# The first modulation's matrix loaded ahead of the latents, and the tokens' norm summed by four groups of 128

## The chip, the cores and the metric

The kernel runs on one core of one Trainium2 chip. The metric is the device time of one execution in microseconds; the time given is the median of three runs. TensorE is called PE here, VectorE DVE, ScalarE ACT, GpSimd POOL and SyncE SP, as in the profile; PEld is PE's loading of weights.

## The reference

One layer of a block with two parallel mixers, for 512 latent tokens and 256 context tokens of width 2048. What stands at the kernel's start is this part:

```python
shift, scale, gate = jnp.split(silu(c) @ w_ada + b_ada, 3, axis=-1)
shift_c, scale_c, gate_c = jnp.split(silu(c_ctx) @ w_ada + b_ada, 3, axis=-1)
h = _rmsnorm(x, norm_g) * (1 + scale) + shift        # 512 x 2048
hc = _rmsnorm(ctx, norm_g) * (1 + scale_c) + shift_c
p = h @ w_in                                          # 2048 -> 9216
...
def _rmsnorm(x, g):
    return x * lax.rsqrt(jnp.mean(x * x, axis=-1, keepdims=True) + EPS) * g
```

Behind it come grouped-query attention over latents and context, a Fourier mix of 512 channels, gates, an output projection, a gated residual add and a last norm.

## The kernel before

Tokens lie along the free dimension, channels along the partitions: the latents are `xt`, 128 x 16 x 512 in f32, that is 16 blocks `kb` of 128 channels. Main products are f32 products made of three fp32r products each (`mm3`, L251 to L253): both operands are split into an upper half (`whi`, made on ACT, L131) and a lower half (`wlo`, made on DVE, L132).

The start works block by block. For block `kb`, `modulation(kb)` forms shift and gain of its 128 channels for latents and context: the two conditioning vectors `c2`, as 32 columns, times the block's columns of `w_ss` (`wa`, two tiles of 1 MB; 16 products at L425, four of them side by side in four groups of 32 columns). `columns` copies the result (L432, ACT), turns it (L435, PE) and adds the four groups up (L439, DVE); shift and gain follow (L487, L488, DVE). `make_h` then forms ht = xt x gain x rx (L414, DVE), its upper half (L415, ACT) and lower half (L416, DVE), and the block's main products with pieces of `w_start` can run (14 groups of three). `rx` is the tokens' inverse root mean square, the same for all channels of a token, kept on all 128 partitions.

`rx` comes from `squares`, called before the first modulation: each block of latents is squared (L394 on ACT, three of them L392 on DVE), pairs of blocks are added (L395, DVE), and eight products with a matrix of ones (L397, f32, 128 x 512) sum over channels into one bank of PSUM. Root (L404, ACT) and reciprocal (L405, DVE) work on 128 x 512. `warm` (L445) issues products whose results nobody reads.

Order is set by the queues. SP issues, in its program's order, the latents, the first modulation's matrix, first pieces of `w_start`, the second modulation's matrix, further pieces; POOL issues the matrices from the third on. `wa` has four buffers and the pieces of `w_start` four (`RAW`), so loads wait until their buffer's last reader is done. Each engine works through its own instructions in a fixed order, which a scheduler sets when the kernel is built. Behind the start everything else follows in the order of the code.

Of the kernel before, what the change touches and what calls it, by code (L numbers as in the profile page):

```python
# [10 lines left out]
F32 = mybir.dt.float32  # L11
F32R = mybir.dt.float32r
ACT = mybir.ActivationFunctionType
ALU = mybir.AluOpType
# [4 lines left out]
P = 128  # L19
D = 2048  # L20
T = 512
C = 256
KK = D // P
# [38 lines left out]
    f = {"P1": "Z5", "P2": "S2", "Q6": "S3", "P7": "S4"}.get(name)  # L62
    return [(f, pc - 1)] if f and g == 0 and pc in (1, 2) else []

XCH = [(0, 2), (2, 2), (4, 4), (8, 4), (12, 2), (14, 2)]


def start_pieces():
# [15 lines left out]
def block_kernel(ctx, tc, xT, ctxT, x, c_row, w_ss, w_gate, vecs, qkg, rope, dft_c, dft_s,  # L84
                 w_start, w_kv, w_m, w_g, w_pab, w_o, final_g, out):
    nc = tc.nc
    sb = lambda name, bufs=1, side="left": ctx.enter_context(tc.tile_pool(name=name, bufs=bufs, side=side))

    def region(name, side="left", **kw):
        st = ExitStack()  # L90
        return st, st.enter_context(tc.tile_pool(name=name, bufs=1, side=side, **kw))
# [18 lines left out]
    def uid(s):  # L110
        cnt[0] += 1
        return f"{s}{cnt[0]}"
# [3 lines left out]
    def slot(pool, shape, dt=F32):  # L116

        n = turns[pool] = turns.get(pool, -1) + 1
        return pool.tile([P] + list(shape), dt, tag=f"s{n % KK}", bufs=1, name=uid("s"))

    def hm_tile(shape, dt, name):
        return slot(hm, shape[1:], dt)

    def bank(shape=(P, 512)):
        return ps.tile(list(shape), F32, tag="b1", bufs=4, name=uid("pb"))

    def bank2():
        return ps.tile([P, 1024], F32, tag="b2", bufs=2, name=uid("pd"))
# [6 lines left out]
    todo, ahead = [], []  # L135
# [16 lines left out]
    def start_load():  # L152

        e = todo[0]
        used = [p for a in ahead for p, _ in a.raws]
        free = [p for p in raw_pools for _ in range(p[1] - used.count(p))]
        if len(e.parts) > len(free) or e.stage == 0 and (not chain or left[e.pc]):
            return False
        todo.pop(0)
        for p, src in zip(free, e.parts):  # L160
            raw = p[0].tile([P, 1024], F32, tag=p[2], bufs=p[3], name=uid("wr"))[:, : e.cols]
            nc.sync.dma_start(raw, src)
            e.raws.append((p, raw))
        if e.stage == 0:
            nc.sync.dma_start(chain[e.pc], e.first)
            left[e.pc] = 1
        ahead.append(e)
        return True
# [89 lines left out]
    ones = const.tile([P, P], F32, name="ones")  # L258
# [3 lines left out]
    eps_t = const.tile([P, 1], F32, name="eps_t")  # L262
# [4 lines left out]
    cvt, bada, ng = small[:, : 2 * KK], small[:, 2 * KK : 5 * KK], small[:, 5 * KK :]  # L267
# [8 lines left out]
    hhi = [None] * KK  # L276
    hlo = [None] * KK
# [51 lines left out]
    for g in range(4):  # L329
        for name in ONE_GROUP:  # L330
            stream_product(name, g, w_g[g], BY_DVE_GATES)
            if g >= 2 and name in DONE:
                half, c = DONE[name]
# [8 lines left out]
    for name in OUT_GROUP:  # L342
        stream_product(name, 4, w_o[1], BY_DVE_OUT)
        if name in DONE:
            half, c = DONE[name]
            stream(("x", half, 2 + c), flat(x[half, 2 + c]), 1024, 1, "raw")
    for name in ONE_GROUP:
        stream_product(name, 5, w_o[0], BY_DVE_OUT)
        half, c = {"P2": (0, 0), "P7": (1, 1), "Q3": (1, 0)}.get(name, (0, 0))
# [12 lines left out]
    pa, pap = region("pa", "right")  # L362
    xt = pap.tile([P, KK, T], F32, name="xt")

    def wada_load(kb, h):
        w = pap.tile([P, 8, 256], F32, tag="wada", bufs=4, name=uid("wa"))
        (nc.gpsimd if kb > 1 else nc.sync).dma_start(w, w_ss[kb, :, 8 * h : 8 * h + 8, :])
        return w

    for a, n in XCH:  # L370
        nc.sync.dma_start(xt[:, a : a + n, :], xT[:, a : a + n, :])


    c2 = pap.tile([P, KK, 32], F32, name="c2")
    nc.vector.memset(c2, 0.0)
    rt = pap.tile([P, 1], F32, name="rt")
    ce = pap.tile([P, 2 * KK], F32, name="ce")
    nc.scalar.activation(ce, cvt, ACT.Exp, scale=-1.0)
    nc.scalar.activation(rt, ce[:, 0:1], ACT.Sqrt)
    nc.vector.tensor_scalar(ce, ce, 1.0, None, op0=ALU.add)  # L380
    nc.vector.reciprocal(ce, ce)
    nc.vector.tensor_tensor(c2[:, :, 0:2].rearrange("p k j -> p j k"),
                            cvt.rearrange("p (j k) -> p j k", j=2),
                            ce.rearrange("p (j k) -> p j k", j=2), op=ALU.mult)
    def squares(srcs, n, r, new, run=None):

        acc = bank2()
        for q in range(0, KK, 2):
            a, b = new(), new()
            for t, src in zip((a, b), srcs(q)):  # L390
                if run is None and t is b and q in (4, 8, 10):
                    nc.vector.tensor_tensor(t, src, src, op=ALU.mult)  # L392
                else:
                    nc.scalar.activation(t, src, ACT.Square)  # L394
            nc.vector.tensor_tensor(a, a, b, op=ALU.add)  # L395
            if run is None:
                nc.tensor.matmul(acc[:, :n], ones, a, start=q == 0, stop=q == KK - 2)  # L397
            elif q == 0:
                nc.vector.tensor_copy(run, a)
            else:  # L400
                nc.vector.tensor_tensor(run, run, a, op=ALU.add)
        if run is not None:
            nc.tensor.matmul(acc[:, :n], ones, run, start=True, stop=True)
        nc.scalar.activation(r, acc[:, :n], ACT.Sqrt, bias=eps_t[:, 0:1], scale=1.0 / D)  # L404
        nc.vector.reciprocal(r, r)  # L405

    wada = {(0, h): wada_load(0, h) for h in range(2)}
    while todo and len(ahead) < 3:
        start_load()
    wada.update({(1, h): wada_load(1, h) for h in range(2)})  # L410

    def make_h(hi, lo, src, rr, kb, j, pool, n):
        tmp = pool.tile([P, n], F32, tag="htmp", bufs=2, name=uid("ht"))
        nc.vector.scalar_tensor_tensor(tmp, src, gain[:, kb, j : j + 1], rr, op0=ALU.mult, op1=ALU.mult)  # L414
        nc.scalar.activation(hi, tmp, ACT.Identity, bias=shift[:, kb, j : j + 1])  # L415
        nc.vector.scalar_tensor_tensor(lo, tmp, shift[:, kb, j : j + 1], hi.bitcast(F32),  # L416
                                       op0=ALU.add, op1=ALU.subtract)

    def matvec(acc, pieces):

        kk = 0
        for w in pieces:
            for k in range(w.shape[1]):
                j = kk % 4
                nc.tensor.matmul(acc[32 * j : 32 * j + 32, :256], c2[:, kk, :], w[:, k, :],  # L425
                                 start=kk < 4, stop=kk >= KK - 4)
                kk += 1

    def columns(acc, kb):

        o = pap.tile([P, 256], F32, tag="ada_o", bufs=2, name=uid("ado"))
        nc.scalar.copy(o, acc[:, :256])  # L432
        sp = acc[:, 512:768]
        for i in range(2):
            nc.tensor.transpose(sp[:, P * i : P * i + P], o[:, P * i : P * i + P], ident)  # L435
        if kb == 0:
            warm(5, o)
        r = pap.tile([P, 2, 2], F32, tag="ada_r", bufs=2, name=uid("adr"))
        nc.vector.tensor_reduce(r, sp.rearrange("p (h g r) -> p h r g", h=2, g=4)[:, :, 0:2, :], axis=AX.X, op=ALU.add)  # L439
        return r  # L440

    def warm(n, src):

        for _ in range(n):
            nc.tensor.matmul(wacc[:, :256], ones, src, start=True, stop=True)  # L445
# [35 lines left out]
    def modulation(kb):  # L481
        acc = bank2()
        matvec(acc, pieces := [wada.pop((kb, h), None) or wada_load(kb, h) for h in range(2)])
        if kb == 0:
            warm(3, pieces[1][:, 7, :])
        sp = columns(acc, kb)
        nc.vector.tensor_scalar(shift[:, kb, :], sp[:, 0, :], bada[:, kb : kb + 1], None, op0=ALU.add)  # L487
        nc.vector.tensor_scalar(gain[:, kb, :], sp[:, 1, :], bsc1[:, kb : kb + 1], ng[:, kb : kb + 1],  # L488
                                op0=ALU.add, op1=ALU.mult)

    wacc = bank()
    rx = pap.tile([P, T], F32, name="rx")
    squares(lambda q: (xt[:, q, :], xt[:, q + 1, :]), T, rx, lambda: hm_tile([P, 2, T], F32, name=uid("sq"))[:, 0, :])
    modulation(0)

    work = start_work()
    done = 0
    for kb in range(KK):
        if kb:
            modulation(kb)  # L500
        if kb % 2 == 0:
            pairs.append([hm_tile([P, 2, T], F32R, name=uid(n)) for n in ("hh", "hl")])
        hhi[kb], hlo[kb] = (t[:, kb % 2, :] for t in pairs[-1])
        make_h(hhi[kb], hlo[kb], xt[:, kb, :], rx, kb, 0, pap, T)

        full = max([k + n for k, n in GROUPS if k + n <= kb] or [0])
        owed = 42 * full
        lim = min(owed, done + 48)
        while done < lim:
            done += next(work)  # L510
# [88 lines left out]
    for g in range(4):  # L599
        gate_b(g)  # L600
        positions(g)
        if g < 2:
            channels(g + 2)
    squares(ct_load, C, rc, lambda: crp.tile([P, C], F32, tag="sq", bufs=4, name=uid("sq")),
            crp.tile([P, C], F32, name="run"))
    crs.close()
# [66 lines left out]
    for which, half in ((0, 0), (0, 1), (1, 1)):  # L673
        toks = range(3 * half, 3 * half + 3) if which == 0 else (4, 5)
        b = bank2()
        accs = [b[:, :512], b[:, 512:], bank()]
        for pc in range(8):
# [9 lines left out]
            if keys and pc in (1, 3, 5):  # L687
                a, t = keys.pop(0)
# [3 lines left out]
        for a, t in zip(accs, toks):  # L692
            a = a.rearrange("p (h d) -> p h d", h=4)
# [222 lines left out]
    acc = bank()  # L916
# [70 lines left out]
    for i in range(NSTEP + 2):  # L987
# [9 lines left out]
        if i % 3 > 0 and i < 3 * KK:  # L997
            q = i // 3 * 2 + i % 3 - 1
# [3 lines left out]
        if i % 3 < 2 and i < 3 * KK:  # L1002
            q = i // 3 * 2 + i % 3
# [354 lines left out]
```

## Time and profile before

| | |
|---|---|
| time, median of three runs | 1388.69 us (1388.03 to 1389.51) |
| the profiled execution | 1388.98 us |
| its span, first to last instruction | 1387.2 us |
| instructions | 17607 |
| loaded from HBM | 257.34 MB |
| written to HBM | 25.17 MB |
| mean granted clock of PE | 0.992 |

The profile is of one execution. A row of the timeline gives start, duration, engine, source line, operation, what is written and read, and how many instructions were merged into it; in brackets stands the idle time of the engine ahead of it and what ended it. The durations of PE's products overlap, since products are pipelined: how fast they follow each other is read from their starts. In rows of stretches, each engine's busy time is followed by its number of instructions, then the granted clock of PE, the busy share of the DMA engines, and GB/s. In rows of groups come the shapes, the count, busy us and mean ns of one, and idle time.

### The profile page before, as it was taken

How to read it: one execution, taken by the hardware profiler on the slowest of the kernel's cores; microseconds unless marked ns; L12 is line 12 of the kernel's file. 1: busy time of each engine (PE TensorE's matmuls, PEld its weight loads, DVE VectorE, ACT ScalarE, POOL GpSimd, SP SyncE). 2: the span in 40 equal slices, each digit the busy share in tenths (PEclk: the TensorE clock that was granted, in tenths of full speed). 3: DMA queues.
4: the chain of work that ended last, by engine and by line, in shares of the span. 5: the costliest groups of instructions: out<-in, count | busy, mean ns of one | idle time of the engine just before them, and what ended most of it. 6: DMA issues, size and time to landing. Idle time of an engine off the chain costs nothing. (4 is left out here: it accounts for less than half of the span.)

```text
span 1387.2 us, 17607 instructions
## 1 busy us (share of the span) xinstructions
PE 1351.4 (97%) x6810; PEld 1107.1 (80%) x6810; DVE 910.7 (66%) x1191; ACT 630.1 (45%) x861; POOL 116.8 (8%) x173
## 2 busy tenths in 40 slices
PE   7999999999999999999999999999999999999986
PEld 4667789888888888888887788888888788878865
DVE  5765486767865668656743776665956546487577
ACT  5322253534545454554544555444544224364434
POOL 0110000011100001000001101000010100020100
PEclk9999999999999999999999999999999999999998
DMA  9887453645443335433447998989898844588973
GB/s 384 330 343 263 168 186 108 185 122 186 153 145 113 116 113 161 140 98 121 124 143 271 326 291 239 258 226 258 263 269 296 310 152 136 136 184 274 238 220 131
DMA packets 76115, 283.67 MB, mean 204 GB/s; under 512 B 8704, under 2 KB 9344, under 8 KB 71680
## 3 DMA queue, kind: packets, MB, share of 16 engines
q1 hardware_dynamic: 52848, 185.28, 39.9%
q0 software_dynamic: 18000, 79.71, 21.2%
q10 hardware_dynamic: 5184, 17.57, 3.3%
q8 instruction: 53, 0.87, 0.3%
q14 instruction: 30, 0.25, 0.1%
HBM read 257.34 MB, written 25.17 MB: 204 GB/s over the span
## 5 line engine op out<-in xcount | busy, mean ns | idle before, releaser
L131 ACT ACTIVATE whi<-wr 128x1024 fp32r<-128x1024 f32 x178 | 185.0, 1043 | 292.7 <-PE pb L252 84.0
L132 DVE TENSOR_TENSOR wlo<-wr,whi 128x1024 fp32r<-128x1024 f32 x178 | 213.4, 1202 | 140.7 <-ACT whi L131 140.5
L251 PE MATMUL pb<-s,whi 128*128 128x512 f32 x512 | 206.7, 405 | 0.6 <-ACT s L415 0.6
L252 PE MATMUL pb<-s,whi 128*128 128x512 f32 x512 | 200.6, 392 | 0.1
L253 PE MATMUL pb<-s,wlo 128*128 128x512 f32 x512 | 200.5, 392 | 0.0
L252 PE MATMUL y<-wlo,s 128*128 128x512 f32 x320 | 127.2, 397 | 7.3 <-DVE wlo L132 7.2
L251 PE MATMUL x<-whi,s 128*128 128x512 f32 x324 | 127.3, 393 | 2.2 <-ACT whi L131 1.1
L252 PE MATMUL x<-wlo,s 128*128 128x512 f32 x324 | 127.2, 393 | 1.9 <-DVE wlo L132 1.9
L251 PE MATMUL y<-whi,s 128*128 128x512 f32 x320 | 126.8, 396 | 0.8 <-ACT whi L131 0.6
L253 PE MATMUL x<-whi,s 128*128 128x512 f32 x324 | 126.9, 392 | 0.0
L253 PE MATMUL y<-whi,s 128*128 128x512 f32 x320 | 126.4, 395 | 0.0
L251 PEld LDWEIGHTS pb<-s,whi 128*128 128x128 f32 x512 | 96.1, 188 | 21.7 <-issue 4.1
L253 PEld LDWEIGHTS pb<-s,wlo 128*128 128x128 f32 x512 | 96.1, 188 | 21.1 <-issue 0.4
L252 PEld LDWEIGHTS pb<-s,whi 128*128 128x128 f32 x512 | 96.4, 188 | 17.1 <-DVE s L416 1.0
L131 ACT ACTIVATE whi<-R 128x1024 fp32r<-128x1024 f32 x66 | 69.6, 1058 | 66.6 <-PE x L253 38.4
L132 DVE TENSOR_TENSOR wlo<-R,whi 128x1024 fp32r<-128x1024 f32 x66 | 80.0, 1219 | 20.5 <-ACT whi L131 20.4
L955 ACT ACTIVATE p<-pd,mx 128x768 f32<-128x768 f32 x48 | 43.2, 899 | 84.9 <-DVE mx L953 84.9
L252 PEld LDWEIGHTS y<-wlo,s 128*128 128x128 f32 x320 | 61.2, 191 | 22.9 <-DVE wlo L132 10.2
L251 PEld LDWEIGHTS x<-whi,s 128*128 128x128 f32 x324 | 61.3, 189 | 16.2 <-ACT whi L131 1.5
L252 PEld LDWEIGHTS x<-wlo,s 128*128 128x128 f32 x324 | 61.2, 189 | 15.2 <-DVE wlo L132 2.6
L251 PEld LDWEIGHTS y<-whi,s 128*128 128x128 f32 x320 | 61.1, 191 | 14.5 <-ACT whi L131 1.0
L253 PEld LDWEIGHTS x<-whi,s 128*128 128x128 f32 x324 | 61.3, 189 | 12.8
(270 smaller groups left out, 2663.7 us busy)
## 6 DMA issues: line engine op xcount, KB each, us to landing
wr<-in_w_g SPq DMA_DIRECT2D x80, 512.0 KB, 8.2
wa<-in_w_ss POOLq DMA_DIRECT2D x28, 1024.0 KB, 8.3
wr<-in_w_m SPq DMA_DIRECT2D x44, 512.0 KB, 3.8
wr<-in_w_gate SPq DMA_DIRECT2D x32, 512.0 KB, 3.6
wr<-in_w_pab SPq DMA_DIRECT2D x32, 512.0 KB, 4.3
R<-in_w_g POOLq DMA_DIRECT2D x32, 512.0 KB, 10.1
wr<-in_w_o SPq DMA_DIRECT2D x32, 512.0 KB, 5.2
wr<-in_w_start SPq DMA_DIRECT2D x26, 512.0 KB, 6.4
```

Of the source, the lines that this page charges most:

```text
L131: nc.scalar.activation(hi, src, ACT.Copy)
L132: nc.vector.tensor_tensor(lo, src, hi.bitcast(F32), op=ALU.subtract)
L251: nc.tensor.matmul(o, ah, bh, start=start, stop=False, skip_group_check=cont)
L252: nc.tensor.matmul(o, ah, bl, start=False, stop=False, skip_group_check=cont)
L253: nc.tensor.matmul(o, al, bh, start=False, stop=stop, skip_group_check=cont)
L955: nc.scalar.activation(p, sc[:, :NKEY], ACT.Exp, bias=mx[:, 0:1], accum_out=mx[:, 1:2])
```

## The change

The first modulation's matrix (two tiles of 1 MB) is loaded ahead of the latents; the latents' six loads are cut in other sizes; the second and the third modulation's matrix follow behind them on SP's queue, between pieces of `w_start` (the third was loaded by POOL before). `squares` stays for the context alone. For the tokens a new function, `token_norms`, sums squares in another way: each block's 512 squares are cut in four groups of 128 tokens, each multiplied with 32 columns of ones into its own 32 partitions of one bank, so that the sums fill 128 x 128 in place of 128 x 512; root and reciprocal work on that, and four products with a matrix that picks one row out of 32 spread the result back over 128 x 512. A filler product (`warm`) stands behind the sums of each of the first 14 blocks. The result stays in PSUM (`rx0`, read by the first block's `make_h`) and is copied to `rx` for the others. `modulation(0)` now stands ahead of the norm.

```diff
-XCH = [(0, 2), (2, 2), (4, 4), (8, 4), (12, 2), (14, 2)]
+XCH = [(0, 2), (2, 4), (6, 4), (10, 4), (14, 1), (15, 1)]
...
-        (nc.gpsimd if kb > 1 else nc.sync).dma_start(w, w_ss[kb, :, 8 * h : 8 * h + 8, :])
+        (nc.gpsimd if kb > 2 else nc.sync).dma_start(w, w_ss[kb, :, 8 * h : 8 * h + 8, :])
...
+    wada = {(0, h): wada_load(0, h) for h in range(2)}
     for a, n in XCH:
         nc.sync.dma_start(xt[:, a : a + n, :], xT[:, a : a + n, :])
+    start_load()
+    wada.update({(1, h): wada_load(1, h) for h in range(2)})
+    for _ in range(3):
+        start_load()
+    wada.update({(2, h): wada_load(2, h) for h in range(2)})
...
-    wada = {(0, h): wada_load(0, h) for h in range(2)}
-    while todo and len(ahead) < 3:
-        start_load()
-    wada.update({(1, h): wada_load(1, h) for h in range(2)})
+    def token_norms(rx):
+
+        t = hm_tile([P, 2, T], F32, name=uid("nm"))
+        pick, r = t[:, 0, :].rearrange("p (t c) -> p t c", t=4), t[:, 1, :P]
+        nc.gpsimd.memset(pick, 0.0)
+        for t in range(4):
+            nc.gpsimd.memset(pick[32 * t : 32 * t + 1, t, :], 1.0)
+        acc = bank()
+        for kb in range(KK):
+            if kb % 2 == 0:
+                two = hm_tile([P, 2, T], F32, name=uid("sq"))
+            sq = two[:, kb % 2, :]
+            if kb % 3 == 2 or kb == KK - 2:
+                nc.vector.tensor_tensor(sq, xt[:, kb, :], xt[:, kb, :], op=ALU.mult)
+            else:
+                nc.scalar.activation(sq, xt[:, kb, :], ACT.Square)
+
+            for t in range(4):
+                nc.tensor.matmul(acc[32 * t : 32 * t + 32, :P], ones[:, :32], sq[:, t * P : t * P + P],
+                                 start=kb == 0, stop=kb == KK - 1)
+            if kb < KK - 2:
+                warm(1, sq[:, :256])
+        nc.scalar.activation(r, acc[:, :P], ACT.Sqrt, bias=eps_t[:, 0:1], scale=1.0 / D)
+        nc.vector.reciprocal(r, r)
+        acc = bank()
+        for t in range(4):
+            nc.tensor.matmul(acc[:, t * P : t * P + P], pick[:, t, :], r, start=True, stop=True)
+        nc.scalar.copy(rx, acc)
+        return acc
...
-    squares(lambda q: (xt[:, q, :], xt[:, q + 1, :]), T, rx, lambda: hm_tile([P, 2, T], F32, name=uid("sq"))[:, 0, :])
     modulation(0)
+    rx0 = token_norms(rx)
...
-        make_h(hhi[kb], hlo[kb], xt[:, kb, :], rx, kb, 0, pap, T)
+        make_h(hhi[kb], hlo[kb], xt[:, kb, :], rx if kb else rx0, kb, 0, pap, T)
```

The conditioning vectors' exponential also gets a tile of its own (`ex`), so that the steps behind it on DVE need not wait for the reading that loads ACT's table of roots. In the changed kernel the lines of `modulation`, `columns`, `warm`, `make_h` and what follows them are 26 higher (L425 is L451, L445 is L471, L435 is L461); the norm's sums are L426, its root L430, its reciprocal L431, the products that spread it L434.

How the change moves instructions is shown at three places. First SP's queue from the program's start (`xt` are the latents, `wa` the modulations' matrices, `wr` the pieces of `w_start`). Before:

```order
L371 DMA xt<-in_xT 128x1024 x2
L371 DMA xt<-in_xT 128x2048 x2
L371 DMA xt<-in_xT 128x1024 x2
L367 DMA wa_127<-in_w_ss 128x2048
L367 DMA wa_129<-in_w_ss 128x2048
L162 DMA wr_131<-in_w_start 128x1024
L162 DMA wr_133<-in_w_start 128x256
L162 DMA wr_135<-in_w_start 128x512
L367 DMA wa_137<-in_w_ss 128x2048
L367 DMA wa_139<-in_w_ss 128x2048
L162 DMA wr_262<-in_w_start 128x1024
```

And now:

```order
L367 DMA wa_112<-in_w_ss 128x2048
L367 DMA wa_114<-in_w_ss 128x2048
L372 DMA xt<-in_xT 128x1024
L372 DMA xt<-in_xT 128x2048 x3
L372 DMA xt<-in_xT 128x512 x2
L162 DMA wr_122<-in_w_start 128x1024
L367 DMA wa_124<-in_w_ss 128x2048
L367 DMA wa_126<-in_w_ss 128x2048
L162 DMA wr_128<-in_w_start 128x256
L162 DMA wr_130<-in_w_start 128x512
L162 DMA wr_132<-in_w_start 128x1024
L367 DMA wa_134<-in_w_ss 128x2048
```

The first matrix moved ahead of the latents, and one more matrix (`wa_134` and the one behind it) stands on this queue.

Second PE, from its first product to the first main product (`pd` and `pb` are banks of PSUM, `s` a tile of squares, or in L251 the block's upper half). Before:

```order
L397 MATMUL pd_143<-s_180,ones 128x512
L397 MATMUL pd_143<-s_186,ones 128x512
L425 MATMUL pd_194<-wa_127,c_118 32x256 x8
L425 MATMUL pd_194<-wa_129,c_118 32x256 x8
L445 MATMUL pb_141<-wa_129,ones 128x256 x3
L435 MATMUL pd_194<-ident,ado_214 128x128 x2
L445 MATMUL pb_141<-ado_214,ones 128x256 x5
L425 MATMUL pd_233<-wa_137,c_118 32x256 x8
L251 MATMUL pb_276<-s_227,whi_264 128x512
```

Six more L397 stand ahead of these. Now the first rows are:

```order
L451 MATMUL pd_150<-wa_112,c_138 32x256 x8
L451 MATMUL pd_150<-wa_114,c_138 32x256 x8
L471 MATMUL pb_148<-wa_114,ones 128x256 x3
L461 MATMUL pd_150<-ident,ado_170 128x128 x2
L471 MATMUL pb_148<-ado_170,ones 128x256 x5
L426 MATMUL pb_189<-s_190,ones 32x128 x4
L471 MATMUL pb_148<-s_190,ones 128x256
L426 MATMUL pb_189<-s_190,ones 32x128 x4
```

After twelve more such pairs of L471 and L426, the stretch ends with these rows:

```order
L471 MATMUL pb_148<-s_268,ones 128x256
L426 MATMUL pb_189<-s_281,ones 32x128 x8
L434 MATMUL pb_294<-s_183 128x128 x4
L451 MATMUL pd_306<-wa_124,c_138 32x256 x8
L251 MATMUL pb_347<-s_300,whi_335 128x512
L451 MATMUL pd_306<-wa_126,c_138 32x256 x8
L252 MATMUL pb_347<-s_301,whi_335 128x512
```

The first modulation moved ahead of the sums of squares, whose small products alternate with fillers, and the second half of the second modulation moved up to right behind the first main product.

Third DVE, from the reciprocal to the first block's lower half (`wlo` is the lower half of a piece of weights, `adr` the modulation's sums). Before:

```order
L405 RECIPROCAL rx<-rx 128x512
L132 TENSOR_TENSOR wlo_265<-wr_131,whi_264 128x1024
L439 TENSOR_REDUCE adr_223<-pd_194 128x4
L132 TENSOR_TENSOR wlo_269<-wr_133,whi_268 128x256
L487 TENSOR_SCALAR shift<-adr_223,small 128x2
L488 TENSOR_SCALAR gain<-adr_223,bsc_93,small 128x2
L132 TENSOR_TENSOR wlo_273<-wr_135,whi_272 128x512
L414 SCALAR_TENSOR_TENSOR ht_229<-xt,gain,rx 128x512
L416 SCALAR_TENSOR_TENSOR s_228<-ht_229,shift,s_227 128x512
```

And now:

```order
L421 TENSOR_TENSOR s_281<-xt 128x512
L132 TENSOR_TENSOR wlo_336<-wr_122,whi_335 128x1024
L431 RECIPROCAL s_183<-s_183 128x128
L440 SCALAR_TENSOR_TENSOR ht_302<-xt,gain,pb_294 128x512
L442 SCALAR_TENSOR_TENSOR s_301<-ht_302,shift,s_300 128x512
L132 TENSOR_TENSOR wlo_340<-wr_128,whi_339 128x256
```

The lower half of the first piece now stands ahead of the reciprocal, the other two behind the block's lower half, and shift and gain went up ahead of the squares. On ACT, in the same way, the upper half of that first piece (L131) now stands ahead of the root (L430).

More of the change, by code (lines that the diff above doesn't have):

```diff
@@ L376, in block_kernel @@
     rt = pap.tile([P, 1], F32, name="rt")
+    ex = pap.tile([P, 2 * KK], F32, name="ex")
     ce = pap.tile([P, 2 * KK], F32, name="ce")
-    nc.scalar.activation(ce, cvt, ACT.Exp, scale=-1.0)
-    nc.scalar.activation(rt, ce[:, 0:1], ACT.Sqrt)
-    nc.vector.tensor_scalar(ce, ce, 1.0, None, op0=ALU.add)
+    nc.scalar.activation(ex, cvt, ACT.Exp, scale=-1.0)
+    nc.scalar.activation(rt, ex[:, 0:1], ACT.Sqrt)
+    nc.vector.tensor_scalar(ce, ex, 1.0, None, op0=ALU.add)
     nc.vector.reciprocal(ce, ce)
@@ L384, in block_kernel, with squares @@
                             ce.rearrange("p (j k) -> p j k", j=2), op=ALU.mult)
-    def squares(srcs, n, r, new, run=None):
+    def squares(srcs, n, r, new, run):
         acc = bank2()
@@ L390, in squares @@
             for t, src in zip((a, b), srcs(q)):
[L391 to L394, printed above, removed]
+                nc.scalar.activation(t, src, ACT.Square)
             nc.vector.tensor_tensor(a, a, b, op=ALU.add)
-            if run is None:
-                nc.tensor.matmul(acc[:, :n], ones, a, start=q == 0, stop=q == KK - 2)
-            elif q == 0:
+            if q == 0:
                 nc.vector.tensor_copy(run, a)
@@ L401, in squares @@
                 nc.vector.tensor_tensor(run, run, a, op=ALU.add)
-        if run is not None:
-            nc.tensor.matmul(acc[:, :n], ones, run, start=True, stop=True)
+        nc.tensor.matmul(acc[:, :n], ones, run, start=True, stop=True)
         nc.scalar.activation(r, acc[:, :n], ACT.Sqrt, bias=eps_t[:, 0:1], scale=1.0 / D)
         nc.vector.reciprocal(r, r)
-    wada = {(0, h): wada_load(0, h) for h in range(2)}
-    while todo and len(ahead) < 3:
-        start_load()
-    wada.update({(1, h): wada_load(1, h) for h in range(2)})
+    def token_norms(rx):
[25 more added lines that the diff above has]
+        return acc
     def make_h(hi, lo, src, rr, kb, j, pool, n):
```

## The prediction

> **What bounds the kernel now.** I read first the page's part 1, then busy time by stretches, then the timeline of the first 40 us.
>
> ```profile
> PE 1351.4 (97%) x6810; PEld 1107.1 (80%) x6810; DVE 910.7 (66%) x1191; ACT 630.1 (45%) x861; POOL 116.8 (8%) x173
> 25.60:200.00 174.40, 172.86 (x1091) 127.29 (x1092) 110.86 (x187) 60.50 (x92) 13.50 (x26) 1.00 0.72 265
> ```
>
> TensorE (PE) bounds everything behind the start: in the 174.40 us from its first main product on it is busy for 172.86. So what moves that first product (L251 at 25.61 us) moves the end nearly one for one. The start itself:
>
> ```profile
> 5.18 0.63 ACT L394 ACTIVATE s<-xt 128x512 f32<-128x512 f32 x1 [2.46 <-DMA xt<-in_xT]
> 8.63 8.99 PE L397 MATMUL pd<-s,ones 128*128 128x512 f32 x16 [8.63 <-DVE s L395]
> 13.91 1.15 ACT L394 ACTIVATE s<-xt 128x512 f32<-128x512 f32 x2
> 17.66 0.69 ACT L404 ACTIVATE rx<-pd,eps_t 128x512 f32<-128x512 f32 x1 [2.60 <-PE pd L397]
> 18.38 3.35 DVE L405 RECIPROCAL rx<-rx 128x512 f32<-128x512 f32 x1 [2.59 <-ACT rx L404]
> 18.87 1.07 PE L425 MATMUL pd<-wa,c 128*32 128x256 f32 x16 [0.25 <-DMA wa<-in_w_ss]
> 19.87 1.56 PE L445 MATMUL pb<-wa,ones 128*128 128x256 f32 x6
> 20.00 0.37 ACT L432 COPY ado<-pd 128x256 f32<-128x256 f32 x1 [1.66 <-PE pd L425]
> 20.27 1.89 ACT L131 ACTIVATE whi<-wr 128x1024 fp32r<-128x1024 f32 x3
> 21.27 0.38 PE L435 MATMUL pd<-ident,ado 128*128 128x128 f32 x2
> 21.48 2.32 PE L445 MATMUL pb<-ado,ones 128*128 128x256 f32 x10
> 21.65 1.16 DVE L132 TENSOR_TENSOR wlo<-wr,whi 128x1024 fp32r<-128x1024 f32 x1
> 24.06 0.74 DVE L414 SCALAR_TENSOR_TENSOR ht<-xt,gain,rx 128x512 f32<-128x512 f32 x1
> 24.84 0.72 ACT L415 ACTIVATE s<-ht,shift 128x512 fp32r<-128x512 f32 x1 [2.68 <-DVE ht L414]
> 25.61 0.73 PE L251 MATMUL pb<-s,whi 128*128 128x512 f32 x2 [0.59 <-ACT s L415]
> 28.93 1.07 PE L425 MATMUL pd<-wa,c 128*32 128x256 f32 x16 [0.42 <-DMA wa<-in_w_ss]
> ```
>
> Latents are squared as they land (last at 13.9), VectorE (DVE) then has the reciprocal (3.35), a split of weights and the first modulation's last steps in one row until ht at 24.06. An f32 product shows as two records: eight L397 are x16.
>
> **The part that decides: PE's time for the norm.** The squares' sums become, for each of 16 blocks of latents, four products with 32 columns (L426) and, for the first 14, one filler over the full array (L471, the old L445's shape). The fillers stand between the sums in PE's order, so PE changes between 32-column and full-width work 28 times. What one such change costs stands in the trace:
>
> ```profile
> 17.55 0.42 PE L425 MATMUL pd<-wa,c 128*32 128x256 f32 x4
> 17.79 0.13 PEld L425 LDWEIGHTS pd<-wa,c 128*32 128x32 f32 x4
> 18.00 0.61 PE L425 MATMUL pd<-wa,c 128*32 128x256 f32 x8
> 19.54 0.40 PE L425 MATMUL pd<-wa,c 128*32 128x256 f32 x4
> 19.87 0.48 PE L445 MATMUL pb<-wa,ones 128*128 128x256 f32 x1
> 19.87 0.19 PEld L445 LDWEIGHTS pb<-wa,ones 128*128 128x128 f32 x1 [0.41 <-issue]
> 19.87 0.70 PE L445 MATMUL pb<-wa,ones 128*128 128x256 f32 x2
> 36.87 0.39 PE L251 MATMUL pb<-whi,s 128*128 128x512 f32 x1
> 37.10 0.39 PE L252 MATMUL pb<-wlo,s 128*128 128x512 f32 x1
> 37.32 0.39 PE L253 MATMUL pb<-whi,s 128*128 128x512 f32 x1
> 37.64 1.93 PE L425 MATMUL pd<-wa,c 128*32 128x256 f32 x32
> 39.51 0.50 PE L251 MATMUL pb<-s,whi 128*128 128x512 f32 x1
> 39.84 0.40 PE L252 MATMUL pb<-s,whi 128*128 128x512 f32 x1
> ```
>
> Four 32-column records run side by side as a round; a round of 256 columns takes about 0.22 us (17.55 to 18.00 is two), so one of 128 columns 0.11. Same-width products follow each other at 0.23 (36.87, 37.10, 37.32). From full to 32 columns it is 0.32 (37.32 to 37.64). From 32 columns to full, the load of weights begins 0.33 after the last round (19.54 to 19.87), having idled 0.41; the first filler record then takes 0.32 (the x6 at 19.87 lasts 1.56, its first two 0.70, so 0.215 a record; L435 follows 1.40 after it, which leaves 0.32 for the first). Loads are not drawn ahead across the change. One block of latents: two rounds of 128 columns apart by 0.14 (0.11, and the 0.03 by which 17.79 lies behind 17.55 plus 0.22), then 0.22 to the filler (0.33 less 0.11 for the shorter stream), 0.32 in the filler, 0.32 back: **1.00 us**. Streaming alone would be 0.11 x 2 + 0.22 x 2, some 0.64. Latents come faster:
>
> ```profile
> 0.00:5.00 5.00, 0.00 (x0) 0.00 (x0) 0.89 (x6) 1.51 (x2) 0.68 (x6) 1.00 0.57 173
> 5.00:10.00 5.00, 1.37 (x2) 0.82 (x3) 2.38 (x6) 4.73 (x9) 0.00 (x0) 1.00 1.02 419
> 10.00:15.00 5.00, 5.00 (x10) 2.04 (x9) 4.51 (x8) 4.00 (x8) 0.00 (x0) 1.00 1.02 424
> ```
>
> At 419 GB/s a block (0.26 MB) takes 0.63. The first 0.86 MB pass by 5.0, and the first latents (0.57 MB with the vectors) are used at 5.18, so use lags the bytes by some 0.8. The first modulation's two halves (1.10 and 2.15 MB) are thus there at 6.4 and 8.9, the last latents, at the same 6.34 MB in all as before, near 18.8, their squares by 19.9.
>
> **When PE can begin.** In PE's order the first modulation and its fillers, moved whole ahead of the sums, stand first: L425's second half to the end of ten fillers, 18.87 to 23.65 (21.48, nine pitches and one stream of 0.22), 4.8 us. Now it starts at 8.9 on a cold array:
>
> ```profile
> 11.35 0.34 PEld L397 LDWEIGHTS pd<-s,ones 128*128 128x128 f32 x1 [0.52 <-DVE s L395]
> 12.20 0.29 PEld L397 LDWEIGHTS pd<-s,ones 128*128 128x128 f32 x1 [0.52 <-issue]
> 12.74 0.19 PEld L397 LDWEIGHTS pd<-s,ones 128*128 128x128 f32 x1 [0.24 <-issue]
> 13.17 0.19 PEld L397 LDWEIGHTS pd<-s,ones 128*128 128x128 f32 x1 [0.24 <-issue]
> ```
>
> The pitch halves from 0.85 to 0.43 near 12.3, 3.6 us after PE's first product at 8.63 (the granted clock reads 1.00 throughout, so it does not show this). Full pace from 12.4, 3.5 us into the new row: 3.5 us do 1.75 us of work, 3.05 remain, PE is free at **15.4**. Opening at 10.0 (3.6 after the first half) gives 14.3; at 13.4 gives 16.0. The Trainium skill, "TensorE: Matmul & The Clock Gate", Part 1 (the HAM clock gate), says that the array runs at half rate until a window of some 3.4 us was busy, and that these windows run free of the kernel's start. The trace's 3.6 fits; by the page alone the opening could come up to a window later, which as an estimate adds under 2 us.
>
> **The chain, and the sum.** 14 blocks at 1.00: 29.4. The last two without filler are four rounds at 0.14, the last record lasting 0.27 (see L435 below): 30.1. Root of 128x128: between nothing and 0.69, taken at 0.25 by the nearest rows (0.37 for 256 elements, 0.69 for 512): 30.4. The reciprocal:
>
> ```profile
> L381 DVE RECIPROCAL ce<-ce 128x32 f32<-128x32 f32 x1 | 0.4, 353 | 0.0
> L435 PE MATMUL pd<-ident,ado 128*128 128x128 f32 x10 | 2.0, 277 | 0.0
> ```
>
> From 0.35 at 32 elements and 3.35 at 512, a line gives 0.95 at 128 (bounds 0.35 and 3.35): 31.4 with handoffs of 0.05. L434's four products, eight records at L435's pitch of 0.11 (0.38 less 0.27), the last lasting 0.27: 32.5. Then ht 0.75 and its rounding 0.73, with handoffs: L251 at **34.1, 8.5 later**.
>
> Costs beside this: the 0.6 us copy of rx runs beside ht, and without that cover would add 0.6. Five memsets of GpSimd (POOL) run while it idles, before any root; uncovered, under 1 us. Eight DVE adds (L395), the old sums and 2.4 us of reciprocal go, but what is late next is PE's row, so nothing is credited. On ScalarE (ACT) and DVE the first weights' split now stands ahead of root and reciprocal; those weights are next on the queue behind 18.8, so it is done near 22.5, hidden under PE's row to 30.1 (if PE were early it would cost, see below). The SP queue takes two more issues of 1 MB, behind them the second block's pieces, needed near 45; POOL's remaining loads still wait for the modulation two before. At 0.42 MB a us behind 18.8, the second matrix lands near 25 (2.6 MB more with the first weights) and the third near 32 (3.0 more); PE needs them at 32.8 and 45.
>
> That gives something back. The first block's products took 25.61 to 37.64, 12.03. Now half a modulation fills the wait for the lower half, and no load is late (28.93 waited 0.42): 0.32 to it, 1.00 through it (as 18.87 to 19.87), 0.33, 39 pitches of 0.225, 0.32 out, transposes 0.2: 11.0, **1.0 less** (bounds 0 and 1.3).
>
> Sum: 8.5 - 1.0 = +7.5. The profiled execution took 1388.98 (span 1387.2), 0.29 above the median shown, 1388.69. Forecast **1396.5**. Its own bounds: start -1.1/+0.6, blocks 0.92 to 1.10 us (-1.1/+1.4), chain and give-back +-1.3: 1393 to 1399.8.
>
> **Rivals.**
> 1. Loads are drawn ahead: the blocks take 0.64, 14 x 0.36 = 5.0 less, 1391.5. Against it stand the idle loads at 19.87 and the 0.32 steps; for it, that same-width loads do overlap. The Trainium skill, "TensorE: Matmul & The Clock Gate", section "Step-by-step: what each phase is for", says weights are loaded ahead of running products where row groups do not conflict or the spare weight buffer is the target; by that the change of width would be free, which the 0.41 idle does not bear out.
> 2. Not slower: latents, not PE, pace the norm. Squares end at 19.9, the split (ACT from 20.2, 1.05; DVE to 22.4) holds root and reciprocal, then reciprocal 23.4, L434 24.5, ht 25.3, L251 26.05: +0.45 - 1.0, 1388.4. It decides only if PE needs under (19.9 - 15.4) / 16 = 0.28 us a block, below its 0.64 of streaming.
> 3. The array stays at half pace, since a third of each block is idle: the row of 4.8 takes 9.6 (18.5), blocks 2.0, the two blocks behind and L434 twice as long, L251 some 18.5 later still: 1415. After 12.3 the trace shows no return to the 0.85 pitch, though gaps of half a microsecond occur.
>
> **How the numbers follow.** Forecast 0.77, rival 1 0.12, rival 2 0.05, rival 3 0.06. A measurement of this kernel can tell about 0.2% (2.8 us) from no change. Slower by that (over 1391.5): the forecast, rival 3 and a little under half of rival 1, 0.87; same 0.11; faster 0.02. The range takes in rival 1 and leaves out rivals 2 and 3 and thin ends: 1391 to 1400.
>
> **What would show it.** Right: L426 starts near 15.4, repeats each 1.0 us with fillers between, ends near 30; DVE and ACT idle from 22.5 until the root near 30; L251 near 34; no DMA wait before L451's next halves; PE dense from there. Wrong: L426 blocks at 0.6 us, a root right behind the split near 21, fillers at 0.85, or a hole in PE past 36.

## The result, and the profile after

| | before | after |
|---|---|---|
| time, median (range; runs) | 1388.36 us (1386.47 to 1389.51; 4) | 1401.77 us (1399.64 to 1403.79; 4) |
| ratio to before, with its 95% interval | | 1.0095 (1.0078 to 1.0112) |
| the profiled execution, its span | 1388.98, 1387.2 | 1402.09, 1400.3 |
| products of PE (records) | 6810 | 6958 |

The changed kernel is slower, as forecast, but by 13.1 us between the profiled executions in place of 7.5; its median lies 1.77 above the top of the range. First the page's row of PE and a stretch of 174.40 us from the first main product on, to be held against the same length before:

```profile
PE 1360.0 (97%) x6958; PEld 1112.8 (79%) x6958; DVE 905.9 (65%) x1185; ACT 628.9 (45%) x860; POOL 117.1 (8%) x176
34.95:209.35 174.40, 173.30 (x1095) 128.41 (x1096) 112.62 (x190) 61.63 (x95) 13.24 (x25) 1.00 0.69 250
```

PE is as dense there as before (173.30 against 172.86), so nothing is lost in this stretch. The start, picked rows of the changed kernel's timeline (start, duration, engine, line, operation, what is written and read, instructions merged, and in brackets the idle time ahead and its end):

```profile
6.58 1.94 PE L451 MATMUL pd<-wa,c 128*32 128x256 f32 x16 [6.58 <-DMA wa<-in_w_ss]
8.97 1.93 PE L451 MATMUL pd<-wa,c 128*32 128x256 f32 x16 [0.45 <-DMA wa<-in_w_ss]
...
13.36 2.32 PE L471 MATMUL pb<-ado,ones 128*128 128x256 f32 x10
...
15.61 0.43 PE L426 MATMUL pb<-s,ones 128*32 128x128 f32 x8
15.97 0.30 PEld L471 LDWEIGHTS pb<-s,ones 128*128 128x128 f32 x2 [0.20 <-issue]
15.97 0.70 PE L471 MATMUL pb<-s,ones 128*128 128x256 f32 x2
16.60 0.42 PE L426 MATMUL pb<-s,ones 128*32 128x128 f32 x8
16.95 0.70 PE L471 MATMUL pb<-s,ones 128*128 128x256 f32 x2
...
29.40 0.64 PE L426 MATMUL pb<-s,ones 128*32 128x128 f32 x16
30.11 0.37 ACT L430 ACTIVATE s<-pb,eps_t 128x128 f32<-128x128 f32 x1 [8.75 <-PE pb L426]
30.52 0.95 DVE L431 RECIPROCAL s<-s 128x128 f32<-128x128 f32 x1 [7.90 <-ACT s L430]
31.61 1.13 PE L434 MATMUL pb<-s 128*128 128x128 f32 x8 [1.57 <-DVE s L431]
...
32.78 0.59 ACT L435 COPY rx<-pb 128x512 f32<-128x512 f32 x1 [2.30 <-PE pb L434]
33.40 0.75 DVE L440 SCALAR_TENSOR_TENSOR ht<-xt,gain,pb 128x512 f32<-128x512 f32 x1 [1.93 <-ACT rx L435]
34.18 0.72 ACT L441 ACTIVATE s<-ht,shift 128x512 fp32r<-128x512 f32 x1 [0.82 <-DVE ht L440]
34.96 0.49 PE L251 MATMUL pb<-s,whi 128*128 128x512 f32 x1 [1.21 <-ACT s L441]
...
48.01 0.50 PE L251 MATMUL pb<-s,whi 128*128 128x512 f32 x1
```

The blocks of the norm follow each other at 0.985 us (15.61, 16.60, and 29.40 after fourteen), paced by PE, with each load of weights idle for 0.20 or 0.33 at a change of width. The first main product comes at 34.96, 9.35 later than before (25.61), the second block's at 48.01, 8.50 later than before (39.51). Held against the kernel before product by product, the lag stays at 8.5 from there to 700 us. So far this is the forecast. The rest comes far behind the start. Stretches of ten us, the kernel before:

```profile
1060.00:1070.00 10.00, 10.00 (x46) 8.28 (x45) 7.80 (x9) 6.43 (x8) 0.00 (x0) 1.00 0.97 338
1070.00:1080.00 10.00, 10.00 (x46) 8.29 (x45) 4.34 (x4) 1.89 (x3) 0.00 (x0) 1.00 0.99 351
1080.00:1090.00 10.00, 8.49 (x30) 6.27 (x29) 5.86 (x5) 4.66 (x5) 0.00 (x0) 0.83 0.72 247
```

And the changed kernel, with its timeline from 1064 us on (`y` is a bank, `wr<-at_d` a piece of the attention's output that is loaded back from HBM):

```profile
1060.00:1070.00 10.00, 7.31 (x27) 5.45 (x27) 6.31 (x7) 3.90 (x4) 0.00 (x0) 0.87 0.51 161
1070.00:1080.00 10.00, 10.00 (x37) 8.01 (x36) 8.64 (x10) 6.10 (x8) 0.00 (x0) 0.79 0.99 334
1080.00:1090.00 10.00, 10.00 (x46) 8.29 (x45) 5.85 (x5) 4.02 (x4) 0.00 (x0) 1.00 0.90 334
```

```profile
1064.63 0.39 PE L253 MATMUL y<-s,s 128*128 128x512 f32 x1
1064.69 1.06 ACT L131 ACTIVATE s<-wr 128x1024 fp32r<-128x1024 f32 x1 [5.79 <-DMA wr<-at_d]
1065.65 1.99 ACT L131 ACTIVATE whi<-wr 128x1024 fp32r<-128x1024 f32 x2
1066.75 0.49 PE L251 MATMUL y<-whi,s 128*128 128x512 f32 x1 [1.73 <-ACT whi L131]
1068.20 0.79 PE L252 MATMUL y<-wlo,s 128*128 128x512 f32 x1 [0.95 <-DVE wlo L132]
1068.79 0.63 PE L253 MATMUL y<-whi,s 128*128 128x512 f32 x1
1069.22 0.63 PE L251 MATMUL y<-whi,s 128*128 128x512 f32 x1
```

PE waits for one load, idles 1.9 and 1.2 us (starts 2.12 and 1.45 apart in place of 0.23), and then runs at a pitch of 0.43 instead of 0.23 until 1074, with the granted clock at 0.87 and 0.79 in the two stretches. The kernel before has a smaller stall of the same sort at 1081 to 1087 (0.83), which the changed one lacks. Along the program the lag goes: 8.5 to 700 us; 10.0 from 800 to 1000 (1.5 of it come at 735, where PE waits for ACT); 11.0 just ahead of the stall; 17.1 behind it; 13.4 after the place where the kernel before stalls; 13.1 at the end. What the experiments had to settle is why 8.5 became 13.1.

### The profile page after: what moved, and what is told of

Its sections match the earlier page's. It is cut to its first block, busy times and chain, and to the rows that moved or that the text cites. A ratio compares the mean times of both kernels' runs of the same rounds, so it can differ in the third digit from the quotient of the medians.

```text
span 1400.3 us, 17904 instructions
## 1 busy us (share of the span) xinstructions
PE 1360.0 (97%) x6958; PEld 1112.8 (79%) x6958; DVE 905.9 (65%) x1185; ACT 628.9 (45%) x860; POOL 117.1 (8%) x176
## 5 line engine op out<-in xcount | busy, mean ns | idle before, releaser
L131 ACT ACTIVATE whi<-wr 128x1024 fp32r<-128x1024 f32 x178 | 185.1, 1043 | 293.1 <-PE pb L252 84.6
L251 PE MATMUL pb<-s,whi 128*128 128x512 f32 x512 | 206.8, 405 | 1.2 <-ACT s L441 1.2
L251 PE MATMUL x<-whi,s 128*128 128x512 f32 x324 | 127.5, 393 | 6.8 <-ACT ev L924 5.7
L251 PE MATMUL y<-whi,s 128*128 128x512 f32 x320 | 126.6, 396 | 2.0 <-ACT whi L131 1.7
L251 PEld LDWEIGHTS pb<-s,whi 128*128 128x128 f32 x512 | 96.2, 188 | 22.2 <-issue 4.1
L131 ACT ACTIVATE whi<-R 128x1024 fp32r<-128x1024 f32 x66 | 69.5, 1058 | 69.0 <-PE x L253 38.0
L251 PEld LDWEIGHTS x<-whi,s 128*128 128x128 f32 x324 | 61.2, 189 | 20.5 <-ACT ev L924 6.1
L251 PEld LDWEIGHTS y<-whi,s 128*128 128x128 f32 x320 | 61.1, 191 | 15.5 <-ACT whi L131 2.2
L253 PEld LDWEIGHTS y<-whi,s 128*128 128x128 f32 x320 | 61.1, 191 | 13.2 <-DVE s L132 0.4
```

The source lines that it names most:

```text
L131: nc.scalar.activation(hi, src, ACT.Copy)
L251: nc.tensor.matmul(o, ah, bh, start=start, stop=False, skip_group_check=cont)
L253: nc.tensor.matmul(o, al, bh, start=False, stop=stop, skip_group_check=cont)
```

## The experiments

"Lag" is how much later the product that the kernel before starts at 90 us starts. Ratios are to runs of the kernel before on the same chip. Times and ratios are medians of several executions, while lags, landings and stalls are read from one profiled execution of each kernel; the executions of one kernel lie up to 9 us apart (1386.01 to 1395.02 without the fillers).

**1. The temporaries' turns.** Temporary tiles are handed out in turn; the norm took 16 before and takes 9 now, so one piece of the attention's output gets another tile, and the splits and loads for it stand later. This kernel advances the turns by the seven that the norm no longer takes, so that everything behind the start has the order of before:

```diff
     rx0 = token_norms(rx)
+    turns[hm] += 7
```

> The changed kernel, with the 16 turning buffers (hm) moved on by the seven turns that the old norm took and the new one doesn't, so that everything behind the start stands in the order of before. Theory S (slots: the seven turns move one piece of attention output and its load back on SP, ACT and DVE near 1060 us, and that costs what is missing behind the start): about 8.5 to 9 us above the kernel before, near 1397, and no extra delay behind 700 us. Rival D (the shifted start meets the transfers differently, or luck): as the changed kernel, near 1402, with the delay growing from 8.6 to 13 behind 700 us. In both the first main product stays near 35.0 us.

Measured: 1404.62 us, ratio 1.0106 (1.0088 to 1.0125). The stall near 1067 is there as in the changed kernel. The order behind the start is not the cause.

**2. The kernel before with the turns of the changed one** (`turns[hm] -= 7` behind its norm).

> The kernel before, with its turning buffers moved back by seven turns and nothing else, so that the loads near 1050 us stand in the order of the changed kernel. Theory S: 3 to 5 us slower than before, near 1392.5, lost behind 1000 us. Rival D: as before, within 1 us of 1388.4. The start is the same in both, first main product at 25.6.

Measured: 1387.38 us, ratio 0.9981 (0.9969 to 0.9994). The same change of order costs nothing, and its profiled execution (1384.26) has no stall at 1081.

**3. No fillers in the norm.**

```diff
-            if kb < KK - 2:
-                warm(1, sq[:, :256])
```

> The changed kernel without the 14 filler products. Theory W (PE's changes between 32 columns and full width make the norm late): a block takes at most 0.3 us, the latents pace the norm, its root starts right behind the split of the first weights near 21.3, the first main product stands near 26 to 27, and the time is 8 to 9 us under the changed kernel, near 1393. Rival C (without fillers the array falls to half pace): the products that spread the norm and the first main ones follow at double pitch, first main product near 27, and 2 to 4 us of the gain are lost again, near 1396. If neither: first main product near 35 as now.

Measured: 1388.44 us, ratio 0.9997 (0.9984 to 1.0011). Its timeline:

```profile
18.22 1.99 PE L426 MATMUL pb<-s,ones 128*32 128x128 f32 x48 [1.02 <-ACT s L423]
20.27 0.37 ACT L428 ACTIVATE s<-pb,eps_t 128x128 f32<-128x128 f32 x1 [0.55 <-PE pb L426]
...
25.80 1.65 PE L251 MATMUL pb<-s,whi 128*128 128x512 f32 x3
27.25 0.44 PE L252 MATMUL pb<-s,whi 128*128 128x512 f32 x1
```

The sums now wait for squares, not for PE, and end 10 us earlier; the first main product is back at 25.80, 0.2 behind the kernel before, though PE's first three then run at half pace. So most of the start's delay came with the fillers (a lag of 1.6 is left of 8.5). The time fell by 13.3, more than the 8 to 9 expected from the start.

**4. Fillers of the sums' own width**, four 32-column products of 256 side by side in place of one over the full array:

```diff
-                warm(1, sq[:, :256])
+                for t in range(4):
+                    nc.tensor.matmul(wacc[32 * t : 32 * t + 32, :256], ones[:, :32], sq[:, :256], start=True, stop=True)
```

> The changed kernel with each filler made of four products with 32 columns of ones (256 columns of the same squares each), so that PE streams as long (0.43 us a filler) without changing width. Theory W: a block takes 0.70 to 0.75 us in place of 0.985, the first main product stands 3.3 to 4 us earlier, near 31.3, and the time is 3 to 4 us under the changed kernel, near 1398. Rival (the block's time is the wait for its square or a fixed cost of each filler): 0.985 a block and no change.

Measured: 1388.93 us, ratio 1.0002 (0.9988 to 1.0017). Its timeline:

```profile
15.44 0.43 PE L426 MATMUL pb<-s,ones 128*32 128x128 f32 x8
15.68 0.61 PE L430 MATMUL pb<-s,ones 128*32 128x256 f32 x8
16.11 0.40 PE L426 MATMUL pb<-s,ones 128*32 128x128 f32 x8
16.33 0.61 PE L430 MATMUL pb<-s,ones 128*32 128x256 f32 x8
...
24.56 0.62 PE L426 MATMUL pb<-s,ones 128*32 128x128 f32 x16
...
30.09 0.49 PE L251 MATMUL pb<-s,whi 128*128 128x512 f32 x1 [0.36 <-ACT s L442]
```

A block takes 0.65 (15.68 to 16.33) in place of 0.985 with as many columns streamed, so 0.33 a block, 4.7 in fourteen, were the changes of width. That is rival 1's price, reached by making the widths equal. The Trainium skill, "TensorE: Matmul & The Clock Gate", section "Step-by-step: what each phase is for", lets loads run ahead of products where row groups do not conflict or the spare weight buffer is the target. By these two kernels that holds where the width stays, and not where it changes. But the total is 12.8 below the changed kernel's (1401.77), where the first main product is only 4.9 earlier: no stall appears near 1060 in this kernel.

**5. A pure delay.** Is it the delay that makes the stall? The kernel before with its five fillers behind the first modulation made fifteen (`warm(5 + 10, o)`), then twenty-five; every engine's order stays.

> The kernel before with ten more fillers (0.43 us each) behind the first modulation on PE, and every order else the same: the first main product should come at about 28.2 us, 2.6 later than in the kernel before. Theory D (a late start alone, however it is made, costs little up to some 4 us and more than itself beyond, because stalls on loads far behind the start absorb it or are deepened by it): 0 to 2.6 later, 1389 to 1392 us. Theory one-for-one: 1391.8. Theory O (what the changed kernel pays behind the start comes from its own order of loads and tiles): 1391.8 at most.

> The kernel before with twenty more fillers: the first main product at about 32.5 us, 6.9 later, the second block's some 6 later, since the first block's wait for its lower half is covered. Theory D: 1399 to 1403, with a stall of PE near 1060 us and a half pace behind it, as in the changed kernel. One-for-one: 1395 to 1396. Theory O: 1395 at most, no stall that the kernel before lacks. If stalls on loads absorb any delay of the start: 1389 to 1391.

Measured: ten more, lag 2.5, 1395.65 us, ratio 1.0061 (1.0047 to 1.0075); twenty more, lag 7.5, 1397.06, ratio 1.0075 (1.0061 to 1.0089). The first main products came at 29.94 and 35.14, later than the 28.2 and 32.5 expected. The smaller delay costs 7.9, three times itself, with the stall of the changed kernel (at 1057.6); 5.0 more cost 1.4, and the kernel with twenty more, which was to have that stall too, loses only 0.7 near 1062 and 1.3 near 1079, both without a half pace. Neither a cost of one for one, nor one that grows with the delay, nor anything in the new code explains that.

**6. The 32-wide fillers with eleven full-width ones ahead**, to bring the start to where the changed kernel has it.

> The kernel with fillers of 32 columns (first main product at 30.1 us, 1388.9 in all) with eleven more fillers of full width ahead of the sums, so that the first main product comes as late as in the changed kernel, at about 34.8. Theory D: 1400 to 1404, as the changed kernel. If PE's changes of width cost something beyond the start: 1393 to 1394. If a delay is absorbed: 1389.

Measured: lag 5.6 (the first main product came at 33.74, not 34.8), 1392.77 us, ratio 1.0036 (1.0024 to 1.0048), no stall near 1060. A start later than that of the ten fillers gives a faster kernel. The theory that a late start alone does it falls.

**7. No fillers, two behind the last sums** (`warm(2, sq[:, :256])` ahead of the root).

> The kernel without the fourteen fillers (1388.4; first main products at half pace from 25.80 to 27.5) with two fillers behind the last sums, so that PE is busy from 20.3 on and reaches full pace near 24: second modulation's half and first products at full pace, 1 to 1.5 us less at 40 us. One-for-one: 1387. If the stalls on loads decide: no difference that can be told from 1388.4.

Measured: 1384.94 us, ratio 0.9982 (0.997 to 0.9993). The first three main products take 0.98 us together, from 25.46 on, in place of 1.65 without the two fillers. It is the fastest kernel here, 0.18% or 2.8 us below the kernel before; its lag is only -0.3, and its profiled execution lacks the stall at 1081, to which most of the rest may be due.

**8. What tells the stalling kernels apart.** The stall begins with the first `wr<-at_d` of this part landing late. Such a load ends with 16 landings, as many as the profile counts DMA engines. In the changed kernel 15 of them come 3.01 to 3.37 us after its issue and one at 4.89. The trace's DMA view of that time, 1059.7 to 1064.7 in the changed kernel, shows a packet of another queue:

```profile
q1 hardware_dynamic: 234, 0.89, 59.9%
q8 instruction: 1, 0.02, 2.1%
...
wr<-at_d SPq DMA_DIRECT2D x1, 512.0 KB, 4.9
```

Queue q8 is a queue of instructions. In the whole run of the kernel before it has these:

```profile
q8 instruction: 53, 0.87, 0.3%
```

That is 0.87 MB in 53 packets of 16 KB. PE has 6810 products and as many loads of weights, 13620; 0.87 MB over 13620 is 64 bytes each, 256 in a packet, and the changed kernel's 13916 give 54, which is what its page has. So I take q8 for PE's own code, fetched every 256 instructions, that is every 128 products with their loads, some 29 us at 0.227 a product. In the changed kernel one fetch starts at 1060.82, 1.04 us behind the load's issue, and takes 1.71. Over all kernels (landing of that first load in us after its issue; "beyond lag" is the difference of the medians less the lag):

| kernel | lag | medians' difference | beyond lag | load landed | fetch beside it |
|---|---|---|---|---|---|
| changed | 8.5 | 13.4 | 4.9 | 4.89 | yes |
| turns put back | 8.8 | 15.4 | 6.6 | 4.85 | yes |
| before, 10 fillers | 2.5 | 7.9 | 5.4 | 5.12 | yes |
| before, 20 fillers | 7.5 | 9.3 | 1.8 | 4.17 | yes |
| before | 0 | 0 | 0 | 3.26 | no |
| before, turns moved | -0.7 | -1.8 | -1.1 | 3.25 | no |
| no fillers | 1.6 | -0.8 | -2.4 | 3.28 | no |
| no fillers, two behind | -0.3 | -2.8 | -2.5 | 3.25 | no |
| 32-wide | 2.1 | -0.3 | -2.4 | 3.27 | no |
| 32-wide, 11 ahead | 5.6 | 5.0 | -0.6 | 3.16 | no |

All four late landings have a fetch beside them and no other has. Where the fetch falls follows from the number of instructions added ahead: counted from the start of the part ahead on PE, it comes at 42.1 us in the kernel before, at 37.8 in the changed kernel (296 more, one distance of 256 and 40), and at 41.4 with the 32-wide fillers and eleven (508 more, nearly two whole distances). So a later start need not stall more. So far this is a correlation. To test it, instructions are added where they cost the changed kernel no time (first main products at 34.85 and 35.06 against 34.96): 32 tiny products as the first thing on PE, which idles there, shift the fetches by 128 instructions, half their distance; 64 shift them by a whole one and leave them, in the program, where they were.

```diff
     wacc = bank()
+    for _ in range(32):
+        nc.tensor.matmul(wacc[0:32, 0:8], ones[:, 0:32], ones[:, 0:8], start=True, stop=True)
```

> The changed kernel with 32 tiny products (32 columns of ones by 8, into the fillers' bank, read by nobody) as the first thing on PE, while it idles: they cost the start nothing, but shift the instructions behind them by 128 records, half of the 256 that separate two fetches of 16 KB on the instruction queue of PE. Theory F (the stall near 1060 us comes from such a fetch that holds one of 16 DMA engines while the first piece of at_d is loaded; PE then idles for 3 us and goes on at half pace): the fetch falls near 1046 and 1075 in place of 1061, the last of the 16 landings is no longer 1.5 us behind the others, and 3 to 6 us go: 1396 to 1399. Theory D (the late start alone): no difference, 1400 to 1405.

> The same with 64 tiny products, that is one whole distance between fetches: everything that the tiny products do at the start is there, but the fetches fall where they fell in the changed kernel. Theory F: the stall near 1060 is back, 1400 to 1405, 3 to 6 above the kernel with 32. If the tiny products help by something else: as with 32.

Measured: 32 give 1395.34 us, ratio 1.0052 (1.0033 to 1.0072); 64 give 1403.27, ratio 1.0104 (1.009 to 1.0118). They differ by 7.9 us; of that 1.2 is there at 90 us (lags 7.5 and 8.7), and it is the same thing at another load. PE waits near 96 us for a load of `wa`: with 32 its last landings come at 96.52, 96.58 and 96.62, with 64 at 96.69, 96.71 and 97.76, a fetch having started at 92.2. The kernel before has this too (88.08, then 89.09, a fetch at 84.4), so the changed kernel's lag of 8.5 does not show it. Stretches and the same load (DMA view of 5 us from its issue on) with 32:

```profile
1060.00:1070.00 10.00, 10.00 (x45) 8.28 (x45) 9.79 (x10) 7.48 (x11) 0.00 (x0) 1.00 0.75 253
1070.00:1080.00 10.00, 9.95 (x44) 7.92 (x43) 7.05 (x8) 5.01 (x6) 0.00 (x0) 1.00 0.94 340
```

```profile
q1 hardware_dynamic: 268, 1.00, 58.2%
...
wr<-at_d SPq DMA_DIRECT2D x1, 512.0 KB, 3.2
```

And with 64:

```profile
1060.00:1070.00 10.00, 7.20 (x24) 5.31 (x24) 5.92 (x6) 4.85 (x5) 0.00 (x0) 0.79 0.55 169
1070.00:1080.00 10.00, 10.00 (x40) 8.17 (x39) 7.17 (x9) 5.55 (x9) 0.00 (x0) 0.86 0.92 346
```

```profile
q1 hardware_dynamic: 231, 0.88, 60.8%
q8 instruction: 1, 0.02, 1.8%
...
wr<-at_d SPq DMA_DIRECT2D x1, 512.0 KB, 5.3
```

With 32 no q8 packet falls there (the fetches start at 1045.7 and 1074.7, where they were expected, which also shows that q8 carries PE's code), the load lands in 3.2, PE keeps 10.00 of 10 us at a clock of 1.00. With 64 packet, late landing, idle time and lowered clock are all back. The same pair on the kernel before with ten more fillers:

> The kernel before with ten more fillers (1395.65, 7.9 above the kernel before with a start only 2.5 later) and 32 tiny products as the first thing on PE. Theory F: the fetch no longer falls on the first load of at_d, the stall of 2.3 us and the half pace behind it go: 1389 to 1392. Theory that any delay of 2.5 us costs 8: 1394 to 1398.

> The same with 64 tiny products, a whole distance between fetches: theory F has the stall back, 1394 to 1398; otherwise as with 32.

Measured: 1393.78 us, ratio 1.0036 (1.0024 to 1.0048), with 32; 1397.16, ratio 1.0063 (1.0045 to 1.0081), with 64. This pair is the weaker one: the executions overlap (1393.38 to 1395.39 and 1394.38 to 1402.33), and the tiny products delay this start (first main products at 30.95 and 31.73 in place of 29.94; lags 2.4 and 4.0), so that 1.6 of the 3.4 us between them are not behind the start. In the traces the large stall goes and comes back here too (load 3.24 and 5.28). But the kernel with 32 is above what was expected: a stall of 1.2 us stays at 1059.6 without a fetch beside the load. There the load was issued later against PE: 36.0 us behind the start of the part ahead of it on PE (its first `y<-whi` at 1018.33, the load at 1054.31). In the kernels without a stall there it is 31.3 to 33.7, in the changed one 36.7, with 32 tiny products 33.7. So two things add up in the stall: loads issued some 1 to 3 us later against PE, and a fetch beside the load, which takes 1 to 2 more. The kernels show each alone. Issued late without a fetch beside it (36.0, ten fillers and 32 tiny products), the load costs 1.6 us of lag there; a fetch beside it without the late issue (33.8, twenty fillers), 0.7; both (36.4, ten fillers and 64), 5.2, and 6.1 in the changed kernel. The pair on the changed kernel shows that the time of issue too hangs on where the fetches fall (33.7 with 32, 35.5 with 64; between 850 and 1025 us the lag of POOL's loads went from 8.5 to 7.4 and from 9.4 to 11.0). Which loads lose it on the way was not traced.

## Why the prediction was right in the start and wrong in the sum

**The start, term by term.**

| term | forecast | measured |
|---|---|---|
| PE free for the sums | 15.4 | 15.61 |
| a block of latents | 1.00 | 0.985 |
| last sums done, root begins | 30.1 | 30.11 |
| root, with handoff | 0.3 | 0.41 |
| reciprocal, with handoff | 1.0 | 1.09 |
| L434 to ht | 1.1 | 1.79 |
| ht and its rounding, to L251 | 1.6 | 1.56 |
| first main product, later by | 8.5 | 9.35 |
| given back in the first block | 1.0 | 0.85 |
| lag at the second block | 7.5 | 8.50 |

*PE's row.* Right, and for the reason given: the changes of width are the price, as the 32-wide fillers show by taking 0.33 of them away in each block. Full pace ahead of the sums (ten records in 2.32 at 13.36), no return to half pace during the sums (rival 3), DVE and ACT idle (7.90 and 8.75) until the root: all as the text asked for. The weights' split and the loads were hidden.

*The copy of rx.* The text put it "beside ht". The row at 33.40 says that ht waited for it: DVE's 1.93 of idle time ends with ACT's copy, which reads the same bank. That is the 0.6 named as the price without cover, and most of the 0.85 by which the first main product was late against the forecast.

*Rivals.* 1 did not happen in this kernel (0.985, not 0.64). 2 is what the kernel without fillers does: squares pace the norm, first main product 25.80, total unchanged. It needed the fillers gone.

**The step that failed** stands at the front: "what moves that first product ... moves the end nearly one for one". From the second block up to 700 us it did, to a tenth of a microsecond. Behind that the text priced nothing, for or against, and its bounds came from the start alone. The kernel is there at the edge of its loads: the profiled execution before itself loses some 3.6 us at 1081. Where the edge gives way depends on when loads are issued, on when PE needs them, and on where in PE's code a fetch falls. The change moved the fetches with its 296 additional instructions on PE (13916 against 13620): against PE's own work the one fetch came 4.3 us earlier (37.8 in place of 42.1), the first load of `at_d` was issued 3.0 us later (36.7 in place of 33.7), and the two met. One of 16 landings was 1.5 us late. PE lost 3.1 us idle and then some 2.8 at a slow pace (twelve products at 0.43 in place of 0.23, one at 0.59; the granted clock reads 0.50 from 1067.4 to 1074.2). The late issue is the larger part of the load's delay and the late landing the smaller; both go when the fetches are shifted by half a distance. The Trainium skill, "TensorE: Matmul & The Clock Gate", Part 1 (the HAM clock gate), has the array fall back to half rate after about one idle window of 3.4 us. Here 3.57 us with a single product in them were enough, and 2.39 in the kernel before (0.94 and 1.45 at 1081), while 2.51 with ten fillers and 32 tiny products (1.06 and 1.45 at 764) were not; so an empty window of that length was not needed.

With the fetches shifted by half a distance and the start as it is, the changed kernel takes 1395.34, 6.8 above the kernel before in the same runs, near the forecast's 7.5. That nearness is in part luck: the profiled execution with 32 lags by 8.8 just ahead of the place where the kernel before stalls at 1081 and by 5.2 past it, since it has no such stall. Settled is that the places of PE's fetches decide over the stall of the changed kernel, and that stall over most of what the forecast lacked. Open are the 1.5 us at 735, what lets the load's issue fall back against PE, and what makes the kernel before stall at 1081.

## What to carry to other kernels

Fillers that keep PE's clock up belong in the width of the work around them, or behind it: mixed widths cost 0.33 us per pair of changes here, and two fillers behind the sums kept the first main products at full pace, without fourteen between them. Where a program far behind an edit waits closely for its loads, an edit's cost is a local sum plus or minus what that place does, and the place can be moved by the mere number of instructions: before a few us are put down to an edit, compare lags along the program, and repeat the measurement with some idle instructions added at the start. A range for such a kernel has to take in the stalls that the profile before already shows.

## What was not expected of the hardware

One fetch of 16 KB of PE's code held up one of a load's sixteen landings by 1.0 to 2.1 us (4.17 to 5.28 against 3.2), and where that load was also issued 3 us late against PE, this cost the changed kernel 6.1 us; where it was not (twenty fillers), 0.7. A delay of 2.5 us at the start (ten fillers) cost 7.9, one of 5.6 us (32-wide and eleven) 5.0. Tiny products that compute nothing of use, 3.58 us of them in PE's first idle time, made the changed kernel 6.4 us faster (1395.34 against 1401.77), and 7.9 faster than the same with twice as many.
